# Two-layer trunk and stack on one core: weight splits moved to VectorE, and gate projections moved in between the steps of layer 2's gated scan

## The chip, the core and the metric

One core of a Trainium2 chip. The metric is the device time of one execution in microseconds. Three executions of the kernel before took 1567.63, 1570.56 and 1571.66 us; the median is 1570.56 us.

## What is computed

256 tokens of width 1024, with a context of 256 more, go through a first block (a trunk of two layers) and a second block (attention, feed-forward, a recurrent mixer, feed-forward). The change concerns the trunk. Cut to what matters, one trunk layer is:

```python
z, zc = split_columns(prenorm(x) @ w_in), split_columns(prenorm(xc) @ w_in)
y_mla = attention(z, zc) * silu(z['mla_gate'])
y_pool = pool(z) * pool_scale * silu(z['pool_gate'])
y_gla = rmsnorm(gated_scan_both_directions(z, zc)) * silu(z['gla_gate'])
g_mla, g_pool, g_gla = split(sigmoid(z['merge']), 3)
merged = g_mla * (y_mla @ w_bm) + g_pool * (y_pool @ w_bp) + g_gla * (y_gla @ w_bg)
x = x + gate * rmsnorm(merged @ w_out, post_g)
```

The row `gate` is a third of `silu(c) @ mod_w[l] + mod_b[l]` (the "modulation gates" of a layer). The gates `z['gla_gate']` and `z['merge']` depend on the layer's input alone; the products with `w_bg` need the scan's output.

## The kernel before

**A matrix product.** All large products are made of three matmuls with operands of reduced precision (`mm3`, lines 395 to 397): high by high, low by high, high by low. A weight chunk (128 x 1024) is loaded by `raw` (line 361, a DMA on SP's queue into one of three buffers `wr`), copied to its high part `wh` on ScalarE (line 377), and its low part `wl` = `wr` - `wh` is made by a subtraction, the "split" (line 379), on VectorE or on GpSimd: where `lopool[0]` is n and not 0, on GpSimd for every n-th chunk. `wh` and `wl` have three buffers each (`wp`). `win(name, i)` is the projection of the layer's input to 128 columns: one chunk and, in layer 2, 24 matmuls of 256 columns. A branch product (`ws` with the chunk "br") takes 12 such matmuls, with one chunk for two products.

**The trunk's order.** `trunk_core` runs for each layer: first the attention stage (`latents`, `mla`) with pool branch, and in layer 1 modulation columns, as fill; then the gated scan (`gla`). Both are generators, and `weaves` advances the fill by a given ratio for each yield of the main one. `lopool[0]` is 2 within `trunk_core`. In layer 2 the scan has 16 yields for each of two head pairs: sums of the log decays (line 834, 836), the query, key and value projections, a first level, eight levels of decay factors (subtractions in lines 909 to 912, an exponential in 913, the padded query on VectorE and GpSimd in 895, the product with the key on GpSimd in 915, a small matmul in 859), the state, the output, its norm (967 to 974). The fill beside it is a chain: what is left of the pool branch's merge, the MLA gate (`gate_branch("mg", ...)`), the MLA merge (`merge(0, ...)`). `gate_branch` does for each of four tiles: project, silu (lines 451, 452), product with the branch's output (1020), split into the pair `y` (389). `merge` does for each of eight: project, tanh (1030), branch product, sum (1035, or 1037 and 1038), and at the last merge the split into `mo` (389). Pool merge and MLA gate come to an end inside the weave, as do the first of the MLA merge's eight steps; the rest of them are drained behind it.

**The tail of layer 2.** Then come the scan's gate (`gate_branch("gg", ...)`), the last merge (`merge(2, ...)`), and woven with these `mod_gates`: eight 512 KB chunks in four buffers, used unsplit (line 466) into an auxiliary PSUM tile (there are two), a copy (470), a selection matmul (499) and two additions and products with rows (500, 501). Behind them the output projection (`out_proj`), whose chunks go to `wp` and to five more buffers in the pool `hold`.

**Who sets the order.** The program is traced in the order of the emission. A planner then orders the instructions of each engine and DMA queue by priority (the order of the emission, weights up to 300 places earlier) and by a time that it simulates, and assigns the buffers. So a step that is emitted later can run earlier where its operands and a buffer are free.

Of the kernel before, what the change touches and what calls it, by code (L numbers as in the profile page):

```python
# [273 lines left out]
def trunk_and_stack(ctx, tc, xin, w, vec, rows, cst, msk, tabs, toep, out):  # L274
# [9 lines left out]
    def mkpool(stack, name, side=None, space=None):  # L284
        kw = {"space": space} if space else {}
        if side:
            kw["side"] = side
        return stack.enter_context(tc.tile_pool(name=nm(name), bufs=1, **kw))
# [25 lines left out]
    def pair(pl, tag, n1, n2, bufs=1):  # L314
        o = Obj()
        o.h = pl.tile([P, n1, n2], F32R, tag=tag + "h", name=nm(tag + "h"), bufs=bufs)
        o.l = pl.tile([P, n1, n2], F32R, tag=tag + "l", name=nm(tag + "l"), bufs=bufs)
        return o
# [170 lines left out]
    def mod_gates(l, md, pl, *where):  # L489
        sels = [("selx", "gx")] + ([("selc", "gc")] if l == 0 else [])  # L490
        for _, g in sels:
            setattr(md, g, pl.tile([P, D], F32, name=nm(g)))
        for c in range(2):
            mr = yield from mod_rows(l, 4 + c, auxps, *where)
            bB, pB = rowhalf(("mod_b", l), c), rowhalf(("post", l), c)
            for sel, g in sels:
                dst = getattr(md, g)[:, c * 512:c * 512 + 512]
                pg = auxps()
                T.matmul(pg, C(sel), mr, start=True, stop=True)
                V.tensor_tensor(dst, pg, bB, op=OP.add)  # L500
                V.tensor_tensor(dst, dst, pB, op=OP.mult)
        yield
# [131 lines left out]
    def trunk_layer(l, md, xn, M):  # L634
# [381 lines left out]
        def gate_branch(name, src):  # L1016
            M.y = pair(M.lp, "y", 4, TW)
            for i in range(4):
# [2 lines left out]
                split(M.y, (ALL, i), sg, 0.5)  # L1021
                yield

        def merge(b, y, first, mo=None):
            if first:
                M.mg = M.lp.tile([P, 8, TW], F32, tag="mg", name=nm("mg"))
            for f in range(8):
                pg = win("merge", b * 8 + f)
                t = scratch()[:, :TW]
                S.activation(t, pg, AF.Tanh, scale=0.5)  # L1030
                if f % 2 == 0:
                    ch = W(("br", l, b, f // 2))
                pb = ws(ch, y(), 0, TW, 0, (f % 2) * P)
                if first:
                    V.scalar_tensor_tensor(M.mg[:, f, :], t, 1.0, pb, op0=OP.add, op1=OP.mult)
                else:
                    V.scalar_tensor_tensor(t, t, 1.0, pb, op0=OP.add, op1=OP.mult)
                    V.tensor_tensor(M.mg[:, f, :], M.mg[:, f, :], t, op=OP.add)
                if mo is not None:
                    split(mo, (ALL, f), M.mg[:, f, :], 0.5)  # L1040
                yield

        M.latents, M.mla, M.gla, M.gla_kv, M.poolb, M.gate_branch, M.merge = latents, mla, gla, gla_kv, poolb, gate_branch, merge

    def drain(g):
        for _ in g:
            pass
# [30 lines left out]
    def weaves(main, *fills):  # L1078

        acc = [0.0] * len(fills)  # L1080
        for _ in main:
            for i, (g, r) in enumerate(fills):
                acc[i] += r
                while acc[i] >= 1:
                    acc[i] -= 1
                    next(g, None)

    def trunk_core(l, M, modfill):
        lopool[0] = 2
        with ExitStack() as st:  # L1090
            mp = mkpool(st, f"mla{l}")
            pb, m1 = M.poolb(mp), M.merge(1, lambda: M.yp, True)
            fill = chain(lambda: pb, lambda: m1)
            weaves(M.latents(mp), (fill, 0.3))
            weaves(M.mla(mp), (fill, (0.45, 0.7)[l]), (modfill, 0.7))
            drain(pb)
            drain(modfill)
        M.lp2 = mkpool(left, f"og{l}")
        with ExitStack() as st:
            gp = mkpool(st, f"gla{l}")  # L1100
            fill = chain(lambda: m1, lambda: M.gate_branch("mg", lambda: M.ym), lambda: M.merge(0, lambda: M.y, False))
            weaves(M.gla(gp), (fill, 0.45))
            drain(fill)
        lopool[0] = 0


# [97 lines left out]
    with ExitStack() as st:  # L1204
        bd = mkpool(st, "bd")
        mo = pair(bd, "mo", 8, 256)
        with ExitStack() as s2:
            mg1 = mod_gates(1, md1, bd, mkpool(s2, "mods"), 4)
            weaves(chain(lambda: M1.gate_branch("gg", lambda: M1.og), lambda: M1.merge(2, lambda: M1.y, False, mo)), (mg1, 1.0))
            drain(mg1)  # L1210
        rx.close()
        edge = mkpool(right, "edge", side="right")
        hp = ExitStack()
        new_hold(hp)
        xn = pair(xnp, "xna", 8, 256)
        gm = rowvec(edge, ("mpre", 0))
        op = M1.lp.tile([P, 2, D], F32, tag="mg", name=nm("op"))
        out_proj(lambda cb, hf: ("wout", 1, cb, hf), mo, [(t * P, xr[:, t, :], md1.gx) for t in range(2)],
                 [op[:, t, :] for t in range(2)], lambda i: prenorm(xn, i, gm))
# [371 lines left out]
```

## Time and profile before

| | us |
|---|---|
| median of three executions | 1570.56 |
| the profiled execution's own time | 1570.03 |
| its span, first to last instruction | 1568.3 |
| PE busy in the span | 1492.4 (95%) |
| DVE, ACT, POOL busy | 949.9, 756.1, 360.9 |

PE is TensorE, DVE VectorE, ACT ScalarE, POOL GpSimd, SP the engine that issues the DMAs. A busy PE is not PE at its peak: matmuls are pipelined, and their lengths overlap. The clock granted to TensorE is given as a share of full speed. The stages of the trunk lie in the span as follows: layer 1's attention stage 50 to 262 us, its scan to 435, its tail and output projection to 635, layer 2's attention stage to 707, its scan to 836, its tail to 914, with the first output products from 904 on.

### The profile page before, as it was taken

To read this page: it belongs to the slowest core of one execution; us is meant where nothing else is said; L and a number is where in the kernel's file an instruction comes from. 1 tells how busy PE (TensorE), PEld (TensorE's weight loads), DVE (VectorE), ACT (ScalarE), POOL (GpSimd) and SP (SyncE) were. 2 spreads that over 40 slices of the span, in tenths; PEclk is the share of its full clock that TensorE was granted. 3 is DMA by queue.
4 is the path that set the end of the run, shared out by engine and by line. 5 is a ranking of instruction groups with operands and counts; after the bars stand their busy time and mean duration, and the time that the engine had idled before them with its cause. 6 is when DMAs were issued, how large, how long until landed. Compare 5 with 4: busy or idle time off the path is not lost.

```text
span 1568.3 us, 25530 instructions
## 1 busy us (share of the span) xinstructions
PE 1492.4 (95%) x10206; PEld 1284.0 (82%) x10206; DVE 949.9 (61%) x1479; ACT 756.1 (48%) x1267; POOL 360.9 (23%) x276
## 2 busy tenths in 40 slices
PE   6999999999999999998989989989999997899998
PEld 3766668787877789777889989869999887799986
DVE  5555435856445576667694764767665577656654
ACT  4444344453323365755644454554444457534443
POOL 1213125735400002336582020311000034100000
PEclk9999999999999999999999999999999999899999
DMA  8323322222334465224337664425556654435564
GB/s 340 121 103 125 121 90 81 66 76 68 108 110 163 144 189 168 95 74 137 104 133 254 196 217 145 132 85 169 165 186 187 217 187 148 140 130 179 185 187 135
DMA packets 65638, 229.79 MB, mean 147 GB/s; under 512 B 7280, under 2 KB 7920, under 8 KB 65392
## 3 DMA queue, kind: packets, MB, share of 16 engines
q1 hardware_dynamic: 65520, 228.16, 44.9%
q8 instruction: 80, 1.31, 0.3%
q14 instruction: 38, 0.31, 0.1%
HBM read 227.09 MB, written 1.05 MB: 145 GB/s over the span
## 4 chain that ended last, share of the span: by engine, by line
PE 77%; DVE 7%; POOL 4%; issue 4%; DMA 4%; ACT 4%; SPq 0%; POOLq 0%; DVEq 0%; ACTq 0%
PE mm L395 21%; PE mm L397 21%; PE mm L396 21%; DMA wr<-in_w_dram 3%; PE at L735 2%; DVE wl L379 2%; PE aux L768 2%; ACT wh L377 1%; PE at L755 1%; POOL wl L379 1%; POOL E L915 1%; POOL qp L895 1%; PE mm L466 1%; PE at L859 1%; PE aux L466 1%
## 5 line engine op out<-in xcount | busy, mean ns | idle before, releaser
L377 ACT ACTIVATE wh<-wr 128x1024 fp32r<-128x1024 f32 x352 | 370.8, 1055 | 424.9 <-PE mm L396 133.5
L379 DVE TENSOR_TENSOR wl<-wr,wh 128x1024 fp32r<-128x1024 f32 x288 | 363.9, 1265 | 287.2 <-ACT wh L377 285.9
L395 PE MATMUL mm<-xnah,wh 128*128 128x256 f32 (+1 forms) x1192 | 367.9, 309 | 11.2 <-DVE rt L1452 10.3
L397 PE MATMUL mm<-xnah,wl 128*128 128x256 f32 (+1 forms) x1192 | 361.9, 304 | 3.0 <-DVE wl L379 2.1
L396 PE MATMUL mm<-xnal,wh 128*128 128x256 f32 (+1 forms) x1192 | 362.0, 304 | 0.2 <-DVE xnal L386 0.2
L395 PEld LDWEIGHTS mm<-xnah,wh 128*128 128x128 f32 x1192 | 226.6, 190 | 27.8 <-DVE rt L1452 10.6
L379 POOL TENSOR_TENSOR wl<-wr,wh 128x1024 fp32r<-128x1024 f32 (+1 forms) x64 | 158.3, 2473 | 353.3 <-ACT wh L377 268.8
L397 PEld LDWEIGHTS mm<-xnah,wl 128*128 128x128 f32 x1192 | 226.6, 190 | 14.9 <-DVE wl L379 2.7
L396 PEld LDWEIGHTS mm<-xnal,wh 128*128 128x128 f32 x1192 | 226.8, 190 | 10.1 <-issue 1.4
L419 POOL TENSOR_TENSOR sm<-sm,minus_half 128x1 f32<-128x1 f32 (+3 forms) x34 | 25.5, 751 | 628.7 <-DVE sm L567 356.3
L395 PE MATMUL mm<-xnbh,wh 128*128 128x512 f32 (+1 forms) x392 | 138.2, 353 | 0.0
L397 PE MATMUL mm<-xnbh,wl 128*128 128x512 f32 (+1 forms) x392 | 136.9, 350 | 0.0
L396 PE MATMUL mm<-xnbl,wh 128*128 128x512 f32 (+1 forms) x392 | 136.7, 349 | 0.0
L395 PE MATMUL mm<-wh,xnah 128*128 128x256 f32 x288 | 84.3, 294 | 8.5 <-ACT xnah L385 6.3
L395 PEld LDWEIGHTS mm<-xnbh,wh 128*128 128x128 f32 x392 | 75.6, 193 | 11.8 <-issue 2.5
L397 PEld LDWEIGHTS mm<-xnbh,wl 128*128 128x128 f32 x392 | 75.6, 193 | 11.2 <-issue 2.4
L396 PEld LDWEIGHTS mm<-xnbl,wh 128*128 128x128 f32 x392 | 75.7, 193 | 11.0 <-issue 2.1
L396 PE MATMUL mm<-wl,xnah 128*128 128x256 f32 x288 | 83.3, 291 | 1.1 <-POOL wl L379 1.1
L397 PE MATMUL mm<-wh,xnal 128*128 128x256 f32 x288 | 82.6, 290 | 0.7 <-DVE xnal L386 0.7
L396 PE MATMUL mm<-wl,hh 128*128 128x512 f32 x176 | 68.8, 391 | 0.0
L397 PE MATMUL mm<-wh,hl 128*128 128x512 f32 x176 | 68.8, 391 | 0.0
L395 PE MATMUL mm<-yh,wh 128*128 128x512 f32 (+1 forms) x192 | 65.6, 342 | 0.9 <-ACT scr L1030 0.9
(365 smaller groups left out, 2895.5 us busy)
## 6 DMA issues: line engine op xcount, KB each, us to landing
wr<-in_w_dram SPq DMA_DIRECT2D x398, 512.0 KB, 3.6
wr<-in_w_dram SPq DMA_DIRECT2D x18, 256.0 KB, 2.7
row<-in_rows_dram SPq DMA_DIRECT2D x8, 512.0 KB, 5.4
xt<-in_xin_dram SPq DMA_DIRECT2D x4, 512.0 KB, 5.8
scr<-in_rows_dram SPq DMA_DIRECT2D x8, 256.0 KB, 4.8
xr<-in_xin_dram SPq DMA_DIRECT2D x2, 512.0 KB, 4.7
xc<-in_xin_dram SPq DMA_DIRECT2D x2, 512.0 KB, 4.7
toep<-in_toep_dram SPq DMA_DIRECT2D x1, 1024.0 KB, 7.0
```

Of the source, the lines that this page charges most:

```text
L377: S.activation(ch.h, r, AF.Copy)
L379: eng.tensor_tensor(ch.l, r, ch.h.bitcast(F32), op=OP.subtract)
L395: T.matmul(dst, lh, rh, start=first and i == 0, stop=False)
L396: T.matmul(dst, lh, rl, start=False, stop=False)
L397: T.matmul(dst, ll, rh, start=False, stop=last and i == n - 1)
L419: G.tensor_tensor(y, m, minus_half[:, :n], op=OP.pow)
L466: T.matmul(p[32 * j:32 * j + 32, c0:c0 + 256], sc[:, k * 32:k * 32 + 32], r[:, j, :], start=half == 0, stop=half == 1, tile_position=(0, 3 ...
L735: T.matmul(pa[:, :n], qxs[pr, j][:, c0 + qt * P:c0 + qt * P + P], kxs[pr, j][:, :n], start=True, stop=True)
L755: T.transpose(pa[:, k * 256 + qt * P:k * 256 + qt * P + P], r[qt][:, (2 * k2 + k) * P:(2 * k2 + k + 1) * P], ident)
L768: T.matmul(py[64 * j:64 * j + 64, c0:c0 + 256], v[:, k, h * 64:h * 64 + 64], pTs[j][k // 2][:, k % 2, :], start=k == 0, stop=k == nk - 1, ...
L859: T.matmul(pa[c * s:c * s + s, t * 2 * s:(t + 1) * 2 * s], k_[:, i:i + s], q_[:, :, j:j + s], start=True, stop=True, tile_position=(0, c * s))
L895: (V, G)[j].tensor_tensor(b[r, j, :], gq[r], e[r], op=OP.mult)
```

## The change

`lopool[0]` is 0 instead of 2 in `trunk_core`: in both layers all weight splits of attention stage and scan run on VectorE. (The function `load` and the recurrent mixer keep their own ratios.) In layer 2, three things are emitted among the steps of the scan instead of behind it: the scan's gate rows (`gate_pre`: four projections with their silu, kept in `M.sg`), the last merge's gate rows (`merge_pre`: eight projections with their tanh, kept in `M.tg`), and `mod_gates`, now with two chunk buffers. The fill's ratio is 0.82 instead of 0.45, and the MLA merge stands between the two new steps. Behind the scan there remain `gate_post` (four products and splits) and `merge_post` (eight branch products with their sums and splits). `M.sg` and `M.tg` lie in a pool of their own, 12 KB for each partition, which is closed before the pools of the output projection are opened.

```diff
@@ -1021,6 +1021,39 @@
                 split(M.y, (ALL, i), sg, 0.5)
                 yield
 
+        def gate_pre(name, dst):
+
+            for i in range(4):
+                p = win(name, i)
+                t = dst[:, i, :]
+                S.activation(t, p, AF.Tanh, scale=0.5)
+                V.scalar_tensor_tensor(t, t, 1.0, p, op0=OP.add, op1=OP.mult)
+                yield
+
+        def gate_post(sg, src):
+            M.y = pair(M.lp, "y", 4, TW)
+            for i in range(4):
+                V.tensor_tensor(sg[:, i, :], sg[:, i, :], src[:, i, :], op=OP.mult)
+                split(M.y, (ALL, i), sg[:, i, :], 0.5)
+                yield
+
+        def merge_pre(b, dst):
+
+            for f in range(8):
+                S.activation(dst[:, f, :], win("merge", b * 8 + f), AF.Tanh, scale=0.5)
+                yield
+
+        def merge_post(b, tg, y, mo):
+            for f in range(8):
+                if f % 2 == 0:
+                    ch = W(("br", l, b, f // 2))
+                pb = ws(ch, y(), 0, TW, 0, (f % 2) * P)
+                t = tg[:, f, :]
+                V.scalar_tensor_tensor(t, t, 1.0, pb, op0=OP.add, op1=OP.mult)
+                V.tensor_tensor(M.mg[:, f, :], M.mg[:, f, :], t, op=OP.add)
+                split(mo, (ALL, f), M.mg[:, f, :], 0.5)
+                yield
+
         def merge(b, y, first, mo=None):
             if first:
                 M.mg = M.lp.tile([P, 8, TW], F32, tag="mg", name=nm("mg"))
@@ -1041,6 +1074,7 @@
                 yield
 
         M.latents, M.mla, M.gla, M.gla_kv, M.poolb, M.gate_branch, M.merge = latents, mla, gla, gla_kv, poolb, gate_branch, merge
+        M.gate_pre, M.gate_post, M.merge_pre, M.merge_post = gate_pre, gate_post, merge_pre, merge_post
 
     def drain(g):
         for _ in g:
@@ -1086,7 +1120,7 @@
                     next(g, None)
 
     def trunk_core(l, M, modfill):
-        lopool[0] = 2
+        lopool[0] = 0
         with ExitStack() as st:
             mp = mkpool(st, f"mla{l}")
             pb, m1 = M.poolb(mp), M.merge(1, lambda: M.yp, True)
@@ -1097,10 +1131,22 @@
             drain(modfill)
         M.lp2 = mkpool(left, f"og{l}")
         with ExitStack() as st:
-            gp = mkpool(st, f"gla{l}")
-            fill = chain(lambda: m1, lambda: M.gate_branch("mg", lambda: M.ym), lambda: M.merge(0, lambda: M.y, False))
-            weaves(M.gla(gp), (fill, 0.45))
-            drain(fill)
+            if l == 0:
+                gp = mkpool(st, f"gla{l}")
+                fill = chain(lambda: m1, lambda: M.gate_branch("mg", lambda: M.ym), lambda: M.merge(0, lambda: M.y, False))
+                weaves(M.gla(gp), (fill, 0.45))
+                drain(fill)
+            else:
+                pre = mkpool(rx, "pre1", side="right")
+                M.sg = pre.tile([P, 4, 256], F32, name="sg1")
+                M.tg = pre.tile([P, 8, 256], F32, name="tg1")
+                gp = mkpool(st, f"gla{l}")
+                fill = chain(lambda: m1, lambda: M.gate_branch("mg", lambda: M.ym), lambda: M.gate_pre("gg", M.sg),
+                             lambda: M.merge(0, lambda: M.y, False), lambda: M.merge_pre(2, M.tg))
+                mg1 = mod_gates(1, md1, M.lp, mkpool(st, "mods"), 2)
+                weaves(M.gla(gp), (fill, 0.82), (mg1, 0.2))
+                drain(mg1)
+                drain(fill)
         lopool[0] = 0
 
 
@@ -1204,10 +1250,8 @@
     with ExitStack() as st:
         bd = mkpool(st, "bd")
         mo = pair(bd, "mo", 8, 256)
-        with ExitStack() as s2:
-            mg1 = mod_gates(1, md1, bd, mkpool(s2, "mods"), 4)
-            weaves(chain(lambda: M1.gate_branch("gg", lambda: M1.og), lambda: M1.merge(2, lambda: M1.y, False, mo)), (mg1, 1.0))
-            drain(mg1)
+        drain(M1.gate_post(M1.sg, M1.og))
+        drain(M1.merge_post(2, M1.tg, lambda: M1.y, mo))
         rx.close()
         edge = mkpool(right, "edge", side="right")
         hp = ExitStack()
```

## Rows read from the trace of the kernel before

**Rows 1.** The page, parts 4 (shares of the chain) and 5 (costliest groups)

```profile
PE 77%; DVE 7%; POOL 4%; issue 4%; DMA 4%; ACT 4%; SPq 0%; POOLq 0%; DVEq 0%; ACTq 0%
...
L377 ACT ACTIVATE wh<-wr 128x1024 fp32r<-128x1024 f32 x352 | 370.8, 1055 | 424.9 <-PE mm L396 133.5
```

**Rows 2.** Windows: stretch, length, busy PE, PEld, DVE, ACT, POOL (instructions), PEclk, DMA, GB/s

```profile
50.00:262.00 212.00, 211.51 (x1105) 152.34 (x1103) 104.93 (x201) 96.41 (x178) 58.45 (x43) 0.99 0.31 104
262.00:435.00 173.00, 167.53 (x1245) 138.43 (x1235) 105.64 (x135) 74.97 (x110) 88.47 (x53) 0.99 0.26 81
...
707.00:836.00 129.00, 112.70 (x1025) 103.84 (x1024) 95.58 (x149) 73.02 (x127) 85.89 (x67) 0.97 0.39 129
836.00:914.00 78.00, 76.88 (x641) 70.86 (x641) 49.94 (x77) 34.35 (x54) 4.56 (x3) 1.00 0.71 234
914.00:941.00 27.00, 24.07 (x180) 23.08 (x181) 21.11 (x31) 16.59 (x36) 9.02 (x8) 0.94 0.63 216
```

**Rows 3.** Groups of instructions on PE, 707 to 836 us: count, busy, mean, idle before

```profile
L859 PE MATMUL at<-qp,E 128*32 128x64 f32 x192 | 5.8, 227 | 7.4 <-POOL E L915 4.8 <-POOL qp L895 2.6
```

**Rows 4.** The chain of waits, 707 to 845 us: start, length, what

```profile
752.38 0.21 PE mm L395
...
792.73 3.86 POOL wl L379
...
835.03 0.39 ACT og L961
...
837.34 0.12 PE mm L395
840.29 0.44 PE aux L445 x4
```

**Rows 5.** Windows of the split line 379 alone: busy DVE and POOL (instructions), PEclk, DMA

```profile
50.00:262.00 212.00, 17.05 (x12) 28.52 (x13) 0.99 0.31 104
262.00:435.00 173.00, 18.47 (x13) 29.65 (x12) 0.99 0.26 81
635.00:707.00 72.00, 7.47 (x6) 15.93 (x7) 1.00 0.26 81
707.00:836.00 129.00, 19.18 (x14) 36.35 (x15) 0.97 0.39 129
```

**Rows 6.** Groups of instructions on DVE, 707 to 836 us

```profile
L379 DVE TENSOR_TENSOR wl<-wr,wh 128x1024 fp32r<-128x1024 f32 x14 | 19.2, 1370 | 6.9 <-ACT wh L377 6.9
...
L909 DVE TENSOR_TENSOR E<-sum 128x128 f32<-128x128 f32 x16 | 10.4, 648 | 0.0
L910 DVE TENSOR_TENSOR E<-sum 128x128 f32<-128x128 f32 x16 | 10.0, 628 | 0.0
```

**Rows 7.** Groups of instructions on DVE, 836 to 914 us

```profile
L379 DVE TENSOR_TENSOR wl<-wr,wh 128x1024 fp32r<-128x1024 f32 x22 | 26.9, 1224 | 18.2 <-ACT wh L377 18.1
L1038 DVE TENSOR_TENSOR mg<-mg,scr 128x256 f32<-128x256 f32 x13 | 7.7, 589 | 0.1
L1037 DVE SCALAR_TENSOR_TENSOR scr<-scr,mm 128x256 f32<-128x256 f32 x13 | 5.4, 416 | 10.7 <-ACT scr L1030 8.8 <-PE mm L397 1.9
```

**Rows 8.** Line 910 (a decay subtraction) by itself: nanoseconds min/median/max

```profile
L910 DVE TENSOR_TENSOR E<-sum x32: 273/415/2607, 243.7 to 818.9; 128x256 f32<-128x256 f32 x16, 128x128 f32<-128x128 f32 x16
```

**Rows 9.** Who waited for whom on PE, 262 to 435 us: total, times, longest

```profile
PE at L859 <- POOL E L915: 4.0, 3, 2.0
```

**Rows 10.** The chain of waits, 262 to 435 us

```profile
376.23 3.40 DVE wl L379
```

**Rows 11.** Groups of instructions on PE, 836 to 914 us

```profile
L395 PE MATMUL mm<-xnbh,wh 128*128 128x256 f32 x60 | 17.2, 287 | 0.0
...
L395 PE MATMUL mm<-yh,wh 128*128 128x256 f32 x48 | 13.7, 286 | 0.0
```

**Rows 12.** The chain of waits, 836 to 960 us

```profile
876.27 1.43 PE aux L466 x24
...
898.91 4.47 DMA wr<-in_w_dram
```

## The prediction

> **What bounds the kernel now.** I read the chain of waits first: 77% of it is TensorE [rows 1], so the time is TensorE's own work plus the stretches in which TensorE waits or runs at half clock. The table by stages then says where those are. In layer 1's attention stage (50 to 262 us) TensorE is busy 211.5 of 212 us; in layer 1's scan 167.5 of 173; in layer 2's scan (707 to 836) only 112.7 of 129, at a mean granted clock of 0.97; in the tail behind it, 836 to 914, it is 76.9 of 78 [rows 2]. So layer 2's scan has 129 - 112.7 = 16.3 us of idle TensorE, and 0.03 x 129 = 3.9 us lost to clock: 20.2 us that other work could fill. Everything else in the changed stages is nearly full.
>
> What is late in the scan: 7.4 us of the idle time end with a product of GpSimd (the decay factor E or the padded query) on which a small matmul waits [rows 3]. GpSimd's queue holds weight splits ahead of those products; one of 3.86 us stands on the chain itself [rows 4]. [...]
>
> **Part A, the splits go to VectorE.** GpSimd has 13, 12, 7 and 15 weight splits in the attention stage and the scan of layer 1 and those of layer 2 (one that spans an edge counted on both sides); in layer 2's scan they take 36.35 of its 85.89 busy us, 2.4 us each, while VectorE does one in 1.37 us there [rows 2, 5, 6] and in 1.22 us where GpSimd is quiet [rows 7].
>
> GpSimd's other products come sooner by what stood ahead of them. VectorE gets 15 x 1.22 = 18.3 us more in that scan. What speaks for it: a subtraction for the decay takes 0.63 to 0.65 us on average in layer 2's scan [rows 6] and 0.27 us at its shortest [rows 8]; the 32 of these two lines lose 32 x (0.64 - 0.27) = 12 us to something, and the maximum of 2.6 us [rows 8] is of the length of a GpSimd split. [...]
>
> From the rows alone: GpSimd keeps 85.9 - 36.4 = 49.5 us, 42% less, and I take 42% of about 20 us of such lengthening (the two lines' 12 and the two like them at somewhat less) as relief: 8 us.
>
> In layer 1's scan TensorE waited 4.0 us for the product E [rows 9], and a split on VectorE stands on the chain with 3.40 us instead of 1.22 [rows 10]. Of the 5.5 us idle there I take 2.5 as gained. Bounds: 5.5 gained; 4 lost, if three splits come to stand ahead of the score reductions on VectorE in the attention stages, whose TensorE is full and so has no idle time to give. In those two stages I put the change at 0: TensorE's fill covers it, and VectorE is busy 104.9 of 212 us [rows 2]; without that cover each split queued ahead would cost up to 1.22.
>
> **Part B, work that moves from the tail into layer 2's scan.** The scan has 32 yields; 0.45 gave 14 fill steps, 0.82 gives 26. The fill is 6 remaining pool-merge steps, 4 MLA gates, 4 of the new gate rows, 8 of merge 0, 8 of the new merge rows: 30, so 4 merge rows are left behind. The mod gates end inside at 0.2.
>
> The tail now holds 60 x 6 = 360 projection matmuls (15 projections of 24) and 48 x 3 = 144 branch matmuls (12 of 12) [rows 11]. At 0.12 us that is 60.5 us; the mod rows take 64 x 1.43 / 24 = 3.8 and their two selections about 2. Afterwards it holds 4 projections and 8 branch products: 192 matmuls, 23.0 us. So 312 matmuls, 37.4 us, and 5.8 us of mod gates, 43.2 us in all [rows 4, 11, 12], go into the scan. TensorE's work is the same in sum; **the gain is what falls into the 20.2 us, less what the tail loses anew.**
>
> How much is filled? Each moved projection needs a DMA, a copy on ScalarE and a split. ScalarE: 13 more copies of 1.06 us [rows 1] and 12 tanh on 73.0 us of a longer scan [rows 2]: hidden. The DMAs: 13 chunks and 8 mod chunks of 512 KB where the scan moved 129 GB/s and the tail moved 234 [rows 2]: hidden by bandwidth; but SP's queue is in order, the mod rows have two buffers instead of four, and a load that waits for one holds the weight loads behind it, as do the mod gates' four row loads, which wait for scratch. GpSimd gets nothing of what is moved. VectorE: 95.6 now; + 18.3 (part A) + 13 x 1.22 = 15.9 + gate products 4 x 0.42 + merge 0's 4 x (0.42 + 0.59) + six wide mod operations of some 0.8 = 10.7; - 8 relief: 132.5 us [rows 2, 7]. The scan becomes 129 + 43.2 less what is filled. Bounds: nothing filled, or all 20.2. VectorE at 132.5 of some 159 us (83%, now 74%) is busy but not full, and the 7.4 us that hung on GpSimd are the easiest; I take two thirds, **13.5 us**, nearer the upper end.
>
> The mod accumulation holds one of two auxiliary PSUM banks over about ten yields; the scan's outputs and norms use the same two. I put it at 0, covered by fill matmuls; without them each of two ends of a head pair would lose one output copy, under 1 us.
>
> **The tail anew.** After the scan's last output (835.03) the norm needs until 840.29 and on [rows 4]: 4 projections, 11.5 us of TensorE, cover that. Then VectorE has 4 x (0.42 + 0.42) for the gate (a 256-column product and a split, both at line 1037's 0.42), 8 x (0.42 + 0.59 + 0.42) for the merge, 4 branch splits and the first two output splits of 1.22: 3.4 + 11.4 + 7.3 = 22.1 us [rows 7], beside TensorE's 23.0. Two engines with the same load in a chain of short steps don't overlap fully, and before, a merge step had 36 matmuls (4.3 us) to hide it, now 12 (1.4 us against 1.43 on VectorE and half a split). Late next is VectorE. Bounds 1 and 9 us; I take **4**. The chunk that ended late there already waited 4.47 us for its DMA [rows 12]; the tail loses the 4 MB of mod loads, so I don't raise that. The output projection's chunks stand in space that the stored merge rows now hold to the end: a copy and a split, 2.3 us, behind 2.9 us of matmuls on the first two chunks: 0.
>
> **Sum.** 13.5 - 4 + 2.5 = 12.0 us gained. The profiled execution took 1570.03 us around a span of 1568.3, the median is 1570.56, half a microsecond apart: 1570.0 - 12.0 = **1558.0 us**.
>
> **Rivals.**
> - *VectorE becomes the pace (slower).* It decides if GpSimd's remaining 49.5 us and VectorE's 140.5 (no relief) exclude each other: 190 us against a scan of 172. Then a decay subtraction waits behind a split in the 16 rounds of the scan, 16 x 1.22 x one half = 10 us, nothing is filled, and the tail loses 4: about 1584. For it: subtractions of up to 2.6 us, VectorE in order. [...] Against: VectorE and GpSimd now sum to 181 busy us in 129, so they do overlap. Chance 0.19.
> - *Given back in the tail (no change).* 7 us filled and 7 lost behind the scan, where each short merge step waits for its sums, and the clock falls again: about 1570. For it: the stretch behind 914 already has a clock of 0.94 [rows 2]. [...] Chance 0.15.
> - *All is filled.* 20.2 - 2 + 5 = 23: 1547. For it: the idle time is there [rows 2], and the moved projections need nothing of the scan. Chance 0.16.
> - The planner orders instructions by a simulated time, so the part A edit also reshuffles both layers; its sign is open and it is in the range.
>
> **The numbers.** The forecast's own case has 0.50. Faster by over 0.3% (4.7 us, about what a measurement of this kernel can tell from no change) means under 1565.9: 0.16 and nearly all of 0.50 make 0.64. Within: 0.15 and a little of the rest, 0.17. Slower 0.19. The forecast's own range is 1551 to 1566; that of 8 in 10 reaches into the neighbours, 1546 to 1578.
>
> **What would show it.** Right: between the attention stage's end and the output projection 9 to 10 us less in sum; no E or query wait over 1 us at the small score matmuls; layer 2's scan some 155 to 160 us with TensorE idle under 7; clock there 0.99 or more; decay subtractions of layer 2 at 0.5 us or less; the tail some 37 to 40 us to the last merge sum. Wrong: VectorE over 92% busy in the scan with TensorE idle ending at splits; a merge step in the tail of over 2.5 us; SP waiting for mod buffers; the attention stages longer than 212 and 72.

## The result and the profile after

Four executions of the changed kernel took 1546.33 to 1550.93 us, median **1547.74**; the kernel before, on the same chip, 1569.10. The ratio is 0.9864, with a 95% interval of 0.9846 to 0.9881: 21.4 us less, where 12 were forecast. The profiled execution took 1548.55 us. Of the executions in the experiments below one, of part A in layer 1 alone, took 4283.64 us; no time or ratio given here includes it, and why it was slow is not known. The page after, its span and parts 1 and 4 (the last answers to [rows 1]):

```profile
span 1546.7 us, 25517 instructions
...
PE 1485.1 (96%) x10206; PEld 1277.8 (83%) x10206; DVE 955.3 (62%) x1530; ACT 757.8 (49%) x1267; POOL 248.5 (16%) x225
...
PE 81%; DVE 6%; DMA 4%; issue 3%; ACT 3%; POOL 2%; SPq 0%; POOLq 0%; DVEq 0%; ACTq 0%
```

GpSimd's busy time went from 360.9 to 248.5 us, and VectorE's rose only from 949.9 to 955.3 although it took over some fifty splits. The stages, as in [rows 2] (length; busy time of PE, PEld, DVE, ACT, POOL; granted clock; DMA): layer 1's attention stage and scan, layer 2's scan, its tail, its output projection.

```profile
50.00:261.00 211.00, 211.00 (x1114) 152.53 (x1112) 111.51 (x213) 96.36 (x177) 32.60 (x30) 1.00 0.32 104
261.00:431.00 170.00, 166.75 (x1240) 137.96 (x1240) 108.13 (x148) 75.22 (x110) 65.21 (x41) 1.00 0.28 84
...
703.00:858.00 155.00, 151.19 (x1411) 140.41 (x1410) 113.84 (x198) 90.27 (x152) 52.63 (x51) 1.00 0.56 177
858.00:889.00 31.00, 29.65 (x240) 28.57 (x239) 23.79 (x43) 14.88 (x24) 1.01 (x1) 1.00 0.58 189
889.00:917.00 28.00, 23.39 (x172) 22.04 (x172) 18.13 (x28) 15.80 (x32) 6.37 (x5) 0.94 0.61 204
```

Layer 2's scan is longer, as it must be, but TensorE idles 155 - 151.19 = 3.8 us in it instead of 16.3, at a granted clock of 1.00 instead of 0.97. GpSimd is at 52.6 us instead of 85.9. What is left of TensorE's waits there (groups on PE with idle time before them, 703 to 858 us, against [rows 3]):

```profile
L397 PE MATMUL mm<-xnah,wl 128*128 128x256 f32 x123 | 35.9, 292 | 1.4 <-DVE wl L379 1.4
...
L859 PE MATMUL at<-qp,E 128*32 128x64 f32 x192 | 5.8, 225 | 0.0
...
L445 PE MATMUL aux<-ct,sm 128*128 128x128 f32 x4 | 0.8, 285 | 2.4 <-POOL sm L419 2.4
```

The wait of the small score matmuls (line 859) for GpSimd's products, 7.4 us before, is gone. On VectorE, the same stretch, against [rows 6]:

```profile
L379 DVE TENSOR_TENSOR wl<-wr,wh 128x1024 fp32r<-128x1024 f32 x41 | 51.7, 1261 | 31.5 <-ACT wh L377 31.5
L895 DVE TENSOR_TENSOR qp<-gq,E 64x256 f32<-64x256 f32 x16 | 8.8, 555 | 1.7 <-ACT E L913 1.7
...
L909 DVE TENSOR_TENSOR E<-sum 128x128 f32<-128x128 f32 x16 | 6.2, 387 | 0.0
...
L910 DVE TENSOR_TENSOR E<-sum 128x128 f32<-128x128 f32 x16 | 4.7, 294 | 0.0
```

The decay subtractions came down from 0.65 and 0.63 us to 0.39 and 0.29, the split from 1.37 to 1.26, the query product from 0.76 (in the whole scan before) to 0.56. These shorter operations are the larger part of why 113.8 us of VectorE suffice where I had counted 132.5.

The tail, in the chain of waits (start, length, what): first VectorE's short merge steps, then, at the output projection, a load and a GpSimd split. The second block is from the kernel before, where such a load and split stand on the chain at the same place.

```profile
874.45 1.14 DVE wl L379
875.59 0.33 DVE tg L1052
...
886.47 4.58 DMA wr<-in_w_dram
...
892.26 2.36 POOL wl L379
```

```profile
908.69 4.27 DMA wr<-in_w_dram
...
912.95 2.36 POOL wl L379
```

To compare kernels I use four marks in each trace: the first decay product of a scan (the matmul in line 820), the normalization of its last output (line 974), the first matmul of layer 2's output projection, and the end. Each length is from one profiled execution; the medians are of all runs. The kernel before had medians of 1567.93 to 1569.52 us beside the experiments. Where layer 2's scan and tail run the same program, their sums differ by up to 1.5 us between traces (200.8 and 202.0 in two kernels, 183.1 and 184.6 in two others). Lengths in us:

| kernel | layer 1's scan | layer 2's scan | from there to the first output product | both | median of the runs |
|---|---|---|---|---|---|
| before | 211.3 | 137.6 | 63.2 | 200.8 | 1569 |
| changed | 207.6 | 165.0 | 18.1 | 183.1 | 1547.7 |
| part A alone | 207.2 | 128.1 | 64.3 | 192.4 | 1552.8 |
| A in layer 1 alone | 207.2 | 138.8 | 63.2 | 202.0 | 1565.5 |
| part B alone | 212.8 | 181.1 | 17.1 | 198.2 | 1565.4 |
| changed, mod gates behind | 207.2 | 165.9 | 24.6 | 190.5 | 1556.6 |
| changed, fill 0.45 | 207.6 | 133.6 | 57.8 | 191.4 | 1557.7 |
| changed, each split twice | 207.2 | 202.4 | 18.7 | 221.1 | 1586.7 |
| changed, GpSimd subtracts too | 207.2 | 185.2 | 18.1 | 203.3 | 1566.6 |
| changed, GpSimd memsets too | 207.2 | 171.3 | 18.1 | 189.4 | 1553.1 |
| changed, VectorE subtracts too | 207.6 | 182.3 | 15.2 | 197.5 | 1562.6 |
| changed, no split on GpSimd anywhere | 207.2 | 166.5 | 18.1 | 184.6 | 1548.0 |
| changed, layer 2's products on VectorE | 207.2 | 166.6 | 17.5 | 184.1 | 1548.5 |
| changed, both layers' products on VectorE | 202.0 | 166.6 | 17.5 | 184.1 | 1541.8 |

In the changed kernel 17.7 us come from layer 2's scan and tail, 3.7 from layer 1's scan and 0.7 from its attention stage (147.8 to 147.1 us, counted from the first score matmul). The output projection up to its last residual takes 35.4 us instead of 32.2, but this isn't the change's doing as far as the traces tell: with part A in layer 1 alone, where nothing of layer 2 was edited, it takes 35.6, and with the changed kernel's own tail it takes 33.3 to 34.5 in six other runs. What is left, 2 to 3 us, lies in code that is the same, mostly the second block; I don't explain it: over all these traces that block's length differs by more than that.

### The profile page after: what moved, and what is told of

The parts are those of the page before. It is cut to its first block, busy times and chain, and to the rows that moved or that the text cites. A ratio compares the mean times of both kernels' runs of the same rounds, so it can differ in the third digit from the quotient of the medians.

```text
span 1546.7 us, 25517 instructions
## 1 busy us (share of the span) xinstructions
PE 1485.1 (96%) x10206; PEld 1277.8 (83%) x10206; DVE 955.3 (62%) x1530; ACT 757.8 (49%) x1267; POOL 248.5 (16%) x225
## 4 chain that ended last, share of the span: by engine, by line
PE 81%; DVE 6%; DMA 4%; issue 3%; ACT 3%; POOL 2%; SPq 0%; POOLq 0%; DVEq 0%; ACTq 0%
PE mm L395 22%; PE mm L397 22%; PE mm L396 22%; DMA wr<-in_w_dram 3%; PE at L735 2%; DVE wl L379 2%; PE aux L768 2%; ACT wh L377 2%; PE at L755 1%; PE at L859 1%; PE mm L466 1%; POOL wl L379 1%; POOL E L915 1%; POOL qp L895 1%; PE aux L466 0%
## 5 line engine op out<-in xcount | busy, mean ns | idle before, releaser
L379 DVE TENSOR_TENSOR wl<-wr,wh 128x1024 fp32r<-128x1024 f32 x339 | 425.5, 1257 | 340.2 <-ACT wh L377 338.5
L395 PEld LDWEIGHTS mm<-xnah,wh 128*128 128x128 f32 x1192 | 226.9, 190 | 27.4 <-DVE rt L1496 10.5
L397 PEld LDWEIGHTS mm<-xnah,wl 128*128 128x128 f32 x1192 | 226.8, 190 | 17.3 <-DVE wl L379 5.4
L395 PE MATMUL mm<-xnbh,wh 128*128 128x512 f32 (+1 forms) x392 | 135.0, 345 | 0.0
L396 PE MATMUL mm<-yl,wh 128*128 128x512 f32 (+1 forms) x192 | 64.9, 338 | 0.0
```

The lines of the kernel that those rows point to most:

```text
L379: eng.tensor_tensor(ch.l, r, ch.h.bitcast(F32), op=OP.subtract)
L395: T.matmul(dst, lh, rh, start=first and i == 0, stop=False)
L396: T.matmul(dst, lh, rl, start=False, stop=False)
L397: T.matmul(dst, ll, rh, start=False, stop=last and i == n - 1)
```

## The experiments

My theory: layer 2's scan had idle TensorE because GpSimd's splits made its own products late, and moved work fills the rest. Rivals: the planner's chance order; VectorE as the new pace; one part that does it all. Each version below was planned once, so each also carries whatever order the planner gave it.

**Part A alone.** In `trunk_core`, kernel before:

```diff
-        lopool[0] = 2
+        lopool[0] = 0
```

> Part A alone (all splits of both trunk layers on VectorE, nothing moved). The parts add up: layer 1 ends 4.9 us earlier as in the changed kernel, and layer 2's scan, still short of fill, loses its waits for GpSimd's products (7.4 us of idle TensorE before) and some half-clock stretches: 7 to 9 us there, so 12 to 14 us less than the kernel before, near 1556. Rival 1, GpSimd's splits hurt layer 1 alone and part B's fill would have hidden them in layer 2: 5 us less, near 1564. Rival 2, VectorE as the pace: layer 2's scan gets longer, 1566 or more.

Measured: 1552.82 us, ratio 0.9884 (0.9843 to 0.9925), 17 us less where 12 to 14 were expected. Layer 2's scan and tail lost 8.4 us, as expected; layer 1's scan 4.1. So it is not layer 1 alone, and the third case, a longer scan with VectorE as the pace, did not come. VectorE's groups in the scan, 696 to 825 us, and the wait of the small matmuls:

```profile
L379 DVE TENSOR_TENSOR wl<-wr,wh 128x1024 fp32r<-128x1024 f32 x30 | 38.5, 1282 | 17.4 <-ACT wh L377 12.3 <-ACT gsp L946 5.0
...
L909 DVE TENSOR_TENSOR E<-sum 128x128 f32<-128x128 f32 x16 | 5.3, 334 | 0.1
...
L910 DVE TENSOR_TENSOR E<-sum 128x128 f32<-128x128 f32 x16 | 6.2, 387 | 0.0
```

```profile
L859 PE MATMUL at<-qp,E 128*32 128x64 f32 x192 | 6.0, 232 | 3.9 <-POOL E L915 3.9
```

Twice as many splits on VectorE, and each shorter than before (1.28 us instead of 1.37); the subtractions took 0.33 and 0.39 us. The wait for GpSimd halved, from 7.4 to 3.9 us: without the fill not all of it goes.

**Part A in layer 1 alone.**

```diff
-        lopool[0] = 2
+        lopool[0] = 2 * l
```

> Splits on VectorE in layer 1 alone, layer 2 as before. If layer 1's 4.9 us are the split's doing: 4 to 6 us less than the kernel before, with layer 2's scan and tail as long as before (from the first small products on 636 to 640 us to the output projection's start 264 to 266 us). Rival, the 4.9 us are the planner's chance order, another order gives another number: within 2 us of before.

Measured: 1565.48 us, the median of the nine executions, ratio 0.9973 (0.9948 to 0.9998). Layer 1's scan and attention stage are again 4.1 and 0.7 us shorter, while layer 2 stays at 202.0. The median shows 4 of the 4.8 us, nearer to the theory than to the rival. But layer 1's program is the same in all kernels that have part A there, so its equal length (207.2) says nothing against chance: whether another order, with the splits on GpSimd, would do as well was not tried.

**Part B alone.** In the changed kernel:

```diff
-        lopool[0] = 0
+        lopool[0] = 2
```

> Part B alone (rows emitted among the scan's steps, every second split of the trunk still on GpSimd). If the two parts add up: layer 1 as before, layer 2 some 9 us less, near 1560. Rival 1, part B needs part A because GpSimd's splits would be 20 of 2.5 us beside its own products in a scan of 155 us: the scan idles as before, 0 to 4 us less. Rival 2, the fill alone hides GpSimd's lateness: 14 us less in layer 2, near 1555.

Measured: 1565.39 us, ratio 0.9972 (0.9953 to 0.9991), only some 4 us less. Layer 2's scan and tail gain 2.6. **In that stretch most of what part B gains needs part A:** together they give 17.7 us there, where A gives 8.4 and B 2.6 by themselves; 6.7 us exist only together. The whole times don't show this: A's 16.7 and B's 4.1 us add up to 20.8 of 21.4, with A's own interval some 6 us wide to either side, and the traces of A and of B are some 6 and 5 us faster in code that no version changes. Stretch 704 to 886 us, and groups in it on VectorE and on TensorE:

```profile
704.00:886.00 182.00, 170.88 (x1498) 154.29 (x1497) 121.03 (x184) 95.47 (x161) 99.88 (x75) 0.98 0.49 159
```

```profile
L379 DVE TENSOR_TENSOR wl<-wr,wh 128x1024 fp32r<-128x1024 f32 x23 | 31.3, 1360 | 23.5 <-ACT wh L377 23.4
L909 DVE TENSOR_TENSOR E<-sum 128x128 f32<-128x128 f32 x16 | 15.0, 940 | 0.0
```

```profile
L859 PE MATMUL at<-qp,E 128*32 128x64 f32 x192 | 6.9, 227 | 0.0
```

TensorE idles 182 - 170.9 = 11.1 us at a clock of 0.98, with GpSimd at 99.9 us and the first of the four decay subtractions at 0.94 us (the other three at 0.29 to 0.43). But the small score matmuls no longer wait for GpSimd's products, although every second split is on GpSimd again: 8.3 of the 11.1 us end with an operation of VectorE. So the first half of my theory holds only where little fill is at hand. With the fill, in this trace, the splits on GpSimd cost mostly by way of VectorE and hardly by GpSimd's own late products.

**The modulation gates behind the scan again.** In the changed kernel:

```diff
-                mg1 = mod_gates(1, md1, M.lp, mkpool(st, "mods"), 2)
-                weaves(M.gla(gp), (fill, 0.82), (mg1, 0.2))
-                drain(mg1)
+                weaves(M.gla(gp), (fill, 0.82))
...
-        drain(M1.gate_post(M1.sg, M1.og))
-        drain(M1.merge_post(2, M1.tg, lambda: M1.y, mo))
+        with ExitStack() as s2:
+            mg1 = mod_gates(1, md1, bd, mkpool(s2, "mods"), 4)
+            weaves(chain(lambda: M1.gate_post(M1.sg, M1.og), lambda: M1.merge_post(2, M1.tg, lambda: M1.y, mo)), (mg1, 1.0))
+            drain(mg1)
```

> The changed kernel with the modulation gates behind the scan again, woven with the last gate and merge as before, in four buffers. By the theory that TensorE's idle time in the scan is what is filled: 5.8 us of TensorE's work leave a scan that has 3.8 us idle and come back to a tail whose chain is now VectorE's short steps, with room for part of it; 2 to 5 us slower than the changed kernel. Rival, the mod gates in the scan cost what they fill (an auxiliary PSUM bank held for ten yields, SP behind two buffers): 0 to 3 us faster than the changed kernel.

Measured: 1556.63 us, 9 more than the changed kernel (by the ratios to the kernel before, 0.9907 against 0.9864, some 7); more than I expected. The tail grew by 6.5 us (18.1 to 24.6), the whole of the moved work, and the scan did not shrink:

```profile
699.00:865.00 166.00, 159.08 (x1414) 149.60 (x1413) 117.21 (x202) 93.60 (x157) 50.00 (x53) 0.98 0.48 155
```

Idle TensorE went up to 6.9 us there and the clock down to 0.98. So in the scan the mod rows act as fill, and neither the auxiliary bank nor the two buffers cost anything that shows.

**The fill's ratio at 0.45 in the changed kernel.**

```diff
-                weaves(M.gla(gp), (fill, 0.82), (mg1, 0.2))
+                weaves(M.gla(gp), (fill, 0.45), (mg1, 0.2))
```

> The changed kernel with the fill's ratio back at 0.45: 14 of 30 fill steps among the scan's, 16 drained behind it (the mod gates stay in the scan). If the emission order decides when TensorE gets them: the scan ends earlier with TensorE idle 6 to 9 us, and the time is 5 to 8 us above the changed kernel. Rival, the planner pulls free projections forward whatever their place: within 2 us.

Measured: 1557.73 us, 10 more than the changed kernel, where 5 to 8 were expected. Scan and tail take 191.4 us, as with part A alone. The scan, then the tail:

```profile
700.00:834.00 134.00, 125.33 (x1149) 111.75 (x1148) 96.22 (x178) 75.53 (x132) 57.77 (x53) 0.97 0.50 161
834.00:892.00 58.00, 58.00 (x487) 57.52 (x486) 37.63 (x59) 28.10 (x44) 0.00 (x0) 1.00 0.59 182
```

8.7 us idle at 0.97 in the scan, and a full tail. The planner doesn't pull the projections forward by itself; the order of the emission decides.

**Each split of layer 2's scan twice on VectorE.** In `W_`; `twice[0]` is 1 only while layer 2's scan is woven, and the lines that set it are left out here and below:

```diff
+        if twice[0]:
+            V.tensor_tensor(ch.l, r, ch.h.bitcast(F32), op=OP.subtract)
         eng.tensor_tensor(ch.l, r, ch.h.bitcast(F32), op=OP.subtract)
```

> The changed kernel with each weight split of layer 2's scan done twice on VectorE (some 28 to 30 more subtractions of 1.22 us, 35 us in all; VectorE then near 150 busy of 155 us). If VectorE has slack in the scan as its 114 of 155 us say: under half of the 35 us appears, 5 to 15 us slower than the changed kernel. If VectorE is already the pace of the scan: 30 us or more. If only TensorE counts: under 4 us.

Measured: 1586.71 us, 39 more than the changed kernel; the scan alone 37.4, for 40 more subtractions of 1.23 us. My expectation failed: a VectorE that is busy 118 of 165 us had no 35 us to give. GpSimd's query half and two groups on TensorE, 700 to 902 us:

```profile
L898 POOL TENSOR_TENSOR qp<-gq,E 64x256 f32<-64x256 f32 x16 | 29.7, 1854 | 35.2 <-ACT E L916 17.0 <-issue 6.4 <-DVE E L915 5.5
```

```profile
L862 PE MATMUL at<-qp,E 128*32 128x64 f32 x192 | 6.6, 254 | 15.6 <-POOL E L918 14.4 <-DVE qp L898 1.2
...
L400 PE MATMUL mm<-xnah,wl 128*128 128x256 f32 x128 | 38.9, 304 | 2.4 <-DVE wl L382 2.4
```

The waits came back for the most part not at the splits (2.4 us for one group) but at GpSimd's products (14.4), whose query half now took 1.85 us instead of 1.11.

**GpSimd kept busy.** Splits on VectorE as in the changed kernel, but for every second weight chunk of the scan GpSimd subtracts a tile of 128 x 1024 from itself, which nobody reads (`idle[0]`, set to zero once before the scan):

```diff
+        if twice[0] and nlo[0] % 2 == 0:
+            t = idle[0]
+            G.tensor_tensor(t, t, t, op=OP.subtract)
```

> The changed kernel, splits on VectorE, but for every second weight chunk of layer 2's scan GpSimd also subtracts a tile of the same size that nobody reads (some 14 of 2.4 us). This puts back GpSimd's load without a split that comes late. If the load itself hurt (a blocked queue ahead of E and query, and VectorE's two-input operations held up): decay subtractions back at 0.5 us or more and most of part A's layer-2 gain lost, 4 to 9 us slower than the changed kernel. If only the lateness of the split hurt: within 2 us of the changed kernel.

Measured: 1566.64 us, ratio to before 0.9996 (0.9980 to 1.0013): the whole gain gone, 19 us more than the changed kernel where I expected 4 to 9. The stretch 698 to 884 us, VectorE's groups (split, subtractions) and GpSimd's extra one:

```profile
698.00:884.00 186.00, 169.50 (x1489) 154.46 (x1489) 148.29 (x205) 94.27 (x160) 104.03 (x75) 0.97 0.48 155
```

```profile
L381 DVE TENSOR_TENSOR wl<-wr,wh 128x1024 fp32r<-128x1024 f32 x44 | 64.0, 1457 | 28.3 <-ACT wh L379 28.3
...
L914 DVE TENSOR_TENSOR E<-sum 128x128 f32<-128x128 f32 x16 | 9.1, 566 | 0.0
...
L915 DVE TENSOR_TENSOR E<-sum 128x128 f32<-128x128 f32 x16 | 8.0, 498 | 0.0
```

```profile
L384 POOL TENSOR_TENSOR idle<-idle 128x1024 f32<-128x1024 f32 x21 | 48.8, 2323 | 0.9
```

No split of the scan is on GpSimd, and yet the scan is 20 us longer, with VectorE's subtractions back at 0.5 to 0.57 us and its splits at 1.46. So GpSimd's load is enough to lose the gain; the lateness of its splits isn't needed for it. TensorE's longest waits are now for VectorE's splits:

```profile
L402 PE MATMUL mm<-xnah,wl 128*128 128x256 f32 x128 | 38.5, 301 | 5.5 <-DVE wl L381 5.5
```

**Memsets in place of that subtraction.**

```diff
-            t = idle[0]
-            G.tensor_tensor(t, t, t, op=OP.subtract)
+            for _ in range(2):
+                G.memset(idle[0], 0.0)
```

> As the run before with GpSimd kept busy, but its extra work is two memsets of 128 x 1024 (some 1 us each), which read nothing, in place of one subtraction of 2.3 us. If GpSimd's extra work hurts by what it reads beside VectorE's two-input operations: those keep their lengths (subtractions of the decay 0.3 to 0.4 us, splits 1.26) and the time is within 5 us of the changed kernel. If it hurts by standing in GpSimd's queue ahead of E and query: 15 to 20 us slower than the changed kernel, as there.

Measured: 1553.08 us, 5 more than the changed kernel. VectorE's groups, 698 to 865 us, and GpSimd's extra one:

```profile
L381 DVE TENSOR_TENSOR wl<-wr,wh 128x1024 fp32r<-128x1024 f32 x42 | 53.4, 1274 | 30.6 <-ACT wh L379 30.6
...
L914 DVE TENSOR_TENSOR E<-sum 128x128 f32<-128x128 f32 x16 | 5.6, 352 | 0.0
...
L915 DVE TENSOR_TENSOR E<-sum 128x128 f32<-128x128 f32 x16 | 5.1, 321 | 0.0
```

```profile
L384 POOL MEMSET idle<- 128x1024 f32 x42 | 40.1, 954 | 1.8
```

40 us of extra GpSimd time instead of 49, but VectorE's subtractions stay at 0.32 to 0.35 us, and the scan grows by 6.3 instead of 20.2. Standing ahead in GpSimd's queue costs the smaller part; most of the price, some 14 of the 20.2 us, came only with the subtraction, whose two inputs the memsets don't have.

The trace of the kernel before shows the collisions one by one. A decay subtraction (line 910) and the GpSimd split beside it, start and length:

```profile
751.18 2.46 DVE L910 TENSOR_TENSOR E<-sum 128x128 f32<-128x128 f32 x1
```

```profile
751.07 2.42 POOL L379 TENSOR_TENSOR wl<-wr,wh 128x1024 fp32r<-128x1024 f32 x1
```

The subtraction begins after the split and ends 0.15 us behind it, at 753.64. Of the 64 decay subtractions of layer 2's scan, 16 took over 0.5 us, and each of these ended 0.14 to 0.15 us behind a two-input operation of GpSimd, 7 of them behind a split. In the run with the extra subtractions there are 10 such, 6 of them behind an extra one; with the memsets 4, none behind a memset; in the changed kernel 6, all behind GpSimd's products.

**One more subtraction on VectorE, not in the split's way.**

```diff
         eng.tensor_tensor(ch.l, r, ch.h.bitcast(F32), op=OP.subtract)
+        if twice[0]:
+            t = idle[0]
+            V.tensor_tensor(t, t, t, op=OP.subtract)
```

> The changed kernel with one more subtraction of 128 x 1024 on VectorE for each weight chunk of layer 2's scan, on a tile nobody reads: the same load as the split done twice, but no split waits for a second one. If VectorE's load (with GpSimd's products beside it) is what costs: 30 us or more over the changed kernel, as there. If it was the split's lateness: 5 to 15 us.

Measured: 1562.64 us, 15 more than the changed kernel, at the edge of the second case. VectorE's two kinds, 698 to 880 us, and GpSimd's product E:

```profile
L381 DVE TENSOR_TENSOR wl<-wr,wh 128x1024 fp32r<-128x1024 f32 x44 | 54.7, 1246 | 8.1 <-ACT wh L379 8.1
L384 DVE TENSOR_TENSOR idle<-idle 128x1024 f32<-128x1024 f32 x41 | 50.4, 1229 | 2.0 <-POOL idle L1153 1.8
```

```profile
L920 POOL TENSOR_TENSOR E<-E,gk 128x256 f32<-128x256 f32 x16 | 34.6, 2164 | 1.3
```

The same load costs 17.3 us in the scan when no split waits for it, and 37.4 when each does. A little under half of the price is the load, and GpSimd pays part of that: its product E takes 2.16 us instead of 1.25 in the changed kernel.

**GpSimd out of all weight splits**, also those of `load` and of the recurrent mixer:

```diff
-        lopool[0] = 6
+        lopool[0] = 0
...
-        lopool[0] = 3
+        lopool[0] = 0
```

> The changed kernel with GpSimd out of all weight splits (also every sixth chunk of the stored ones and every third in the recurrent mixer). The chain after the change still has GpSimd splits of 2.4 us and more at the output projections and in the mixer: 2 to 6 us less than the changed kernel. Rival, VectorE is the later engine there and gets 11 more splits: 0 to 4 us more.

Measured: 1547.96 us, ratio to before 0.9864 (0.983 to 0.9898), the same as the changed kernel. The 2 to 6 us that I forecast did not come. GpSimd has little else to do at the output projection (6.4 busy us in the 28 from 889 to 917), which may be why; it was not tested.

**The scan's products on VectorE too.** In `gla`, with `X = G if full else V` (layer 2 alone) or `X = V` (both layers):

```diff
-                            (V, G)[j].tensor_tensor(b[r, j, :], gq[r], e[r], op=OP.mult)
+                            (V, X)[j].tensor_tensor(b[r, j, :], gq[r], e[r], op=OP.mult)
...
-                    G.tensor_tensor(e[:, 1, :], e[:, 1, :], kv, op=OP.mult)
+                    X.tensor_tensor(e[:, 1, :], e[:, 1, :], kv, op=OP.mult)
...
-                G.tensor_tensor(ks, ks, gk[:, None, 0:256].to_broadcast([P, 2, 256]), op=OP.mult)
+                X.tensor_tensor(ks, ks, gk[:, None, 0:256].to_broadcast([P, 2, 256]), op=OP.mult)
...
-                G.tensor_tensor(qs, qs, gq[:, None, TW - 256:TW].to_broadcast([P, 2, 256]), op=OP.mult)
+                X.tensor_tensor(qs, qs, gq[:, None, TW - 256:TW].to_broadcast([P, 2, 256]), op=OP.mult)
```

> The changed kernel with layer 2's scan products (E by key, half of the padded query, the two state operands) on VectorE as well, nothing of GpSimd in the scan but the powers and small copies. VectorE gets 16 x (0.41 + 0.41) and some 3 us, 16 us at the lengths without GpSimd, and loses its waits for GpSimd. If what the two engines share is the limit: 0 to 4 us less than the changed kernel (TensorE's idle time there is 3.8 us). Rival, VectorE's queue is the limit: 4 to 12 us more.

> The same in both layers. Layer 1's products are twice as long (some 0.75 us each on VectorE) and TensorE idles 3.3 us in its scan: 0 to 3 us less than with layer 2 alone, or, if VectorE's queue is the limit, 3 to 10 us more.

Measured: layer 2 alone 1548.46 us, ratio 0.9863 (0.9828 to 0.9897), no difference from the changed kernel; both layers **1541.82 us, ratio 0.9818 (0.9791 to 0.9846)**, the lowest of the study and 6.6 us below the version for layer 2 alone, where I expected 0 to 3. Its interval only touches that of the changed kernel, and the four executions of the version for layer 2 alone spread from 1542.78 to 1553.65 us, so the size of this last step is uncertain. In the traces layer 1's scan fell from 207.2 to 202.0 us, of which 1.5 were lost in its tail. First, of the version for both layers, a stretch in layer 1's scan and layer 2's scan between the marks; then layer 2's scan of the changed kernel; then VectorE's groups of the version for both layers, 698 to 860 us:

```profile
261.00:431.00 170.00, 170.00 (x1288) 141.17 (x1287) 112.89 (x181) 76.47 (x111) 7.12 (x10) 1.00 0.27 86
696.00:863.00 167.00, 165.50 (x1490) 150.22 (x1490) 123.08 (x242) 94.90 (x159) 8.87 (x17) 1.00 0.55 174
```

```profile
699.00:864.00 165.00, 161.19 (x1483) 148.60 (x1482) 118.13 (x205) 93.79 (x158) 54.61 (x53) 1.00 0.56 175
```

```profile
L379 DVE TENSOR_TENSOR wl<-wr,wh 128x1024 fp32r<-128x1024 f32 x43 | 52.7, 1227 | 29.3 <-ACT wh L377 29.1
L896 DVE TENSOR_TENSOR qp<-gq,E 64x256 f32<-64x256 f32 x32 | 13.3, 417 | 2.2 <-ACT E L914 2.0
L916 DVE TENSOR_TENSOR E<-E,gk 128x256 f32<-128x256 f32 x16 | 6.6, 424 | 0.4
```

With 36 operations more, 16 products of each kind and four for the state, VectorE is busy 123.1 us between the marks instead of 118.1, because its operations are shorter: a split takes 1.23 us instead of 1.26, a query product 0.42 instead of 0.56. TensorE is busy in all of layer 1's stretch and all but 1.5 us of layer 2's, so there is hardly any idle time left to fill in either scan.

## Why the prediction came out as it did

The sign was right; the size was short by 9 us. 1547.7 us lies within the range of 8 in 10 (1546 to 1578), but below the range of the forecast's own case (1551 to 1566) and next to the rival "All is filled", 1547, which had a chance of 0.16. That rival's terms were not quite met either: 16.4 us were filled, not 20.2, and layer 1 gave 4.4, not 5; its number came close because the tail lost nothing, where it put 2. By the marks, layer 2's scan and tail gave 17.7 us where 13.5 - 4 = 9.5 were forecast, and layer 1 gave 4.4 where 2.5 were. The rest of the 21.4, some 3 us lost in the output projection and as much gained elsewhere, lies in code whose time scatters by that much.

- **Part B's sum, 13.5 us filled of 20.2: right in kind, a little small.** Idle time fell from 16.3 to 3.8 us and the clock's loss from 3.9 to nothing: 16.4 filled. The loss by the clock is in the trace of the kernel before: from 752 to 754 us the granted clock was 0.50, and the matmuls of the chain there start 0.21 us apart instead of 0.12 [rows 4].
- **The tail's 4 us anew: did not come, and this is the largest miss in the sum.** The 18.1 us after the scan, up to the first output product, hold hardly an idle TensorE (29.65 of 31 us busy around it): scan and tail gained 17.7, more than was filled. The output projection behind it was 3.2 us longer in this trace, but that is no loss of the same kind moved on: the chunk that waits 4.58 us for its load and 2.36 for a GpSimd split did so before with 4.27 and 2.36, without any GpSimd split the stage still took 34.2 us, and the same code took 32.2 to 35.6 in kernels that have layer 2 as it was. That TensorE's 23 us in the tail would cover VectorE's 22 so well was not foreseen.
- **Part A's relief, 8 us on VectorE: mis-sized.** I took 42% of the lengthening as gone. The two subtraction lines alone went from 20.4 to 10.9 us, 9.5 of the 12 that I had counted as lost there, where 42% would be 5. VectorE needed 113.8 us in the stretch shown (118.1 between the marks) instead of 132.5, 14 to 19 less (the small terms in that count add up to 10.5, not 10.7; nothing hangs on it). The relief enters the sum only through the two thirds that I took as filled. Part A alone is worth some 17 us of the 21, and the busy kernel lost all of the gain with nothing but extra GpSimd subtractions. I had booked part A in layer 2 as part of the idle time that fill would take; in layer 2's scan and tail it is also the condition for most of what the fill gains (6.7 us only together).
- **Layer 1, 2.5 us: measured 4.4**, inside the bounds of 5.5 gained and 4 lost. The attention stages stayed as they were (147.1 and 64.3 us, before 147.8 and 64.1), as put.
- **The rival "VectorE becomes the pace"** had the right mechanism the wrong way round. The two engines did hold each other up (16 of 64 decay subtractions ended 0.14 to 0.15 us behind an operation of GpSimd), but that was the state before: a split that VectorE does in 1.22 us kept GpSimd, and at times VectorE with it, for 2.4. Its statement "181 busy us in 129, so they do overlap" read waiting as work: the decay subtraction shown above counts 2.46 busy us, 2.31 of them beside a GpSimd split, and line 910 takes 0.27 at its shortest [rows 8]. The runs with extra subtractions and with memsets on GpSimd agree with this reading: the two lines of decay subtractions took 0.5 to 0.57 us in the one and 0.32 to 0.35 in the other, and no long one ended behind a memset. By what the two engines hold each other up, no run shows.
- **"Given back in the tail"** did not come true before the output projection: the granted clock was 1.00 in the tail (858 to 889 us) and 0.94 behind it, as before the change. **The planner's order** was not separated from part A in layer 1; in layer 2 the run with extra subtractions on GpSimd shows that its load alone takes the gain away, though each version is one plan.

## What to carry to other kernels

Where one engine's operations are much longer than its work explains, look for a second engine beside them before trusting its busy share: here GpSimd's splits lengthened VectorE's operations (two lines of decay subtractions took 0.63 and 0.65 us beside them, 0.29 and 0.39 without), and moving work *onto* the busier engine shortened those that were there. Idle time that is to be filled must be made fillable first: in layer 2's scan and tail the moved projections gave 2.6 us alone, and 9.3 with the splits off GpSimd. And what the emission order doesn't offer to the scan, the planner doesn't fetch.

## What the runs showed of the hardware that was not expected

- VectorE's busy time in layer 2's scan rose by only 5 us, 118.1 to 123.1, when 36 GpSimd operations of the scan were moved to it.
- Every decay subtraction of over 0.5 us in layer 2's scan ended 0.14 to 0.15 us behind a two-input operation of GpSimd: 16 of 64 in the kernel before, 6 in the changed one.
- An extra GpSimd subtraction of 2.3 us cost the scan about 1 us for each (21 of them, 20.2 us); two memsets of 0.95 us in its place about 0.3 (6.3 us for 21 pairs).
- At 72% busy, VectorE had no room on the split's path: 40 more subtractions of 1.23 us made the scan 37.4 us longer, and the same number off that path 17.3.
